# Latent attention software-pipelined over job borders: values two key blocks behind the scores, denominators and reciprocals further behind

## The chip, the cores and the metric

The kernel runs on all 8 cores of one Trainium2 chip. Each core takes one latent sequence of 2048 tokens and four prompts of 256 tokens; no core talks to another. The metric is the device time of the slowest core, in microseconds (us).

A program on all eight cores has a slower state, in which one die (cores 0 to 3, or 4 to 7) or both show a lower granted clock and the time is longer. Each run is marked fast or slow, and only fast runs are compared here.

Engines: PE (TensorE matmul), PEld (its weight loads), DVE (VectorE), ACT (ScalarE), POOL (GpSimd), SP (SyncE). The kernel's helper that issues activations is line 101, so exponentials are the `L101` lines that write the tile `wr`.

## The reference, cut to what matters

Two layers: a gated convolution mixer, then grouped-query attention, each followed by a gated feed-forward part. Only the attention of the latent tokens is touched by most of the change: 8 query heads, 2 key heads, 2560 keys (512 cached, 2048 own).

```python
def one_block(qblk):
    s = jnp.einsum('bqkgd,bskd->bkgqs', qblk, kf) * scale
    p = jax.nn.softmax(s, axis=-1)
    return jnp.einsum('bkgqs,bskd->bqkgd', p, vf)
```

## The kernel before

The program is first recorded as operations with the tiles they read and write. A list scheduler then orders each engine's operations by priority and by a simple model of durations, adds the semaphore waits and emits them. Program order fixes the dependencies. Among ready operations on an engine the lower priority number goes first, and for PE that number grows with program order.

Latent queries are handled in two units of 1024 tokens, S0 (the first unit) and S1 (the second). Each unit has 8 jobs of 2 heads and 512 queries, and each job goes through 20 blocks of 128 keys. Per block: two score matmuls into one of two pairs of banks of PSUM, the memory that matmuls write (banks 0-1 and 2-3), one exponential of 1024 columns on ACT into one of 8 buffers, two value matmuls that accumulate into banks 4-5, and on every second block a pair sum on DVE. The pair sums feed the denominators, matmuls with 32 columns of ones into bank 6.

```python
for hd, q0 in jobs:
    ...
    for c in range(nk):                       # nk = 20 key blocks
        b = 2 * (cnt["set"] % 2)              # two pairs of score banks
        ...
        at(P.prio - 5.0, lambda: P.pe(fs, 2 * MM, ..., pk(b, b + 1)), False)      # scores
        P.act(1024, "ps", pk(b, b + 1), pkk, pt, bank(b, 1024), AF.Exp, scale=att_scale)
        P.pe(fv, 2 * MM, pkk + vbk(c), obk)                                       # values
        if c % 2 == 0: first = (pt, pkk)
        else:
            P.dve(... s = s + pt ...); nb.append((s, sk, c))                      # pair sum
        if c in (5, 11, 19):
            at(P.prio + 1.5, lambda: P.pe(fd, ...), False)                        # denominators
        if c == 3 and pend: pend.pop()()                    # normalise the job before
        yield
    P.dve(... tensor_copy(out=osb, in_=bank(ob, 1024)) ...)     # output copy
    P.dve(... reciprocal(out=rc_t, in_=bank(6, 256)) ...)
    ...                                       # split into two bf16 parts, queue norm_o
```

Other work is woven in. The first unit's attention also carries the key, value and query projections of the second unit. The second unit carries the output projection of the first, then its residual and feed-forward norm.

## Time and profile before

| quantity, kernel before | value | view |
|---|---|---|
| median time | 2576.6 us (2575.7 to 2577.9, 4 runs) | times |
| first unit (first score of S0 to first of S1) | 233.2 us | source view of the score line, median of 8 cores |
| second unit (first to last score of S1) | 228.2 us | same |
| an undisturbed job | 23.7 us | timeline |
| clock | 0.988 to 0.992 | cores view |

From the page: the span, the busy time of each engine, and three rows of the table of 40 equal slices, in which a digit is the busy share in tenths.

```profile
span 2577.6 us, 37681 instructions; the slowest of 8 cores (2564.8 to 2577.6 us)
PE 2387.8 (93%) x12981; PEld 1092.1 (42%) x12981; DVE 1600.2 (62%) x1762; ACT 1342.1 (52%) x1831; POOL 1195.5 (46%) x1114
...
PE   1799999999999999999998998988899999999998
...
DVE  0555686666376818753867787496398628746752
ACT  1233443645257535445777887787644435534433
```

A slice is 64.4 us, so the attention lies in slices 22 to 29, and all but one of the eights in PE's row are there. It does not fill PE, and of the other two engines shown only DVE reaches nine there, in one slice. The windows view says the same in us: four stretches are the program up to the first score, the two units, and the rest; columns are start:end, length, then busy time of PE, PEld, DVE, ACT and POOL with instruction counts, granted clock, DMA share and GB/s.

```profile
0.00:1359.70 1359.70, 1241.94 (x6699) 572.34 (x6700) 800.92 (x885) 641.49 (x956) 704.53 (x673) 0.98 0.55 105
1359.70:1592.90 233.20, 210.72 (x1211) 88.52 (x1210) 183.67 (x226) 183.82 (x217) 75.85 (x62) 0.99 0.25 61
1592.90:1823.50 230.60, 203.33 (x1147) 78.10 (x1146) 153.10 (x211) 181.88 (x205) 45.80 (x39) 1.00 0.06 9
1823.50:2577.60 754.10, 731.77 (x3929) 353.19 (x3927) 462.56 (x442) 334.91 (x455) 369.37 (x340) 0.99 0.51 97
```

ACT is busy 184 of 233 us, then 182 of 231, mostly with exponentials. PE's busy time overstates its work: a single matmul of 512 columns is recorded with 0.38 us and a pair with 0.59, so about 0.16 us of every burst is the tail of its last matmul. Who waits for whom is in the chain of waits followed back from the last instruction, here for the two units, as shares by line:

```profile
by line: PE ps L995 21.6%; PE ps L1003 19.4%; ACT wr L101 17.1%; issue 10.2%; PE ps L856 7.2%; PE ps L598 6.4%; DVE wr L1011 4.0%; PE ps L1017 2.9%; PE ps L916 1.5%; DVE rc L1027 1.5%; DMA wr<-wv 1.1%; PE ps L1041 1.0%; DVE ra L1026 0.7%; D
```

L995 are scores, L1003 values, L1017 denominators. The chain alternates between PE and exponentials, and 10% of it is "issue", time in which the engine waited for nothing that the profile shows. The timeline shows where. These are ACT's lines from an undisturbed stretch near the end of the second unit: start, duration, operation, and in brackets how long ACT had been idle and what ended that.

```profile
1765.59 2.95 ACT L101 ACTIVATE wr<-ps 128x1024 bf16<-128x1024 f32 x3 [0.26 <-PE ps L995]
1769.25 2.95 ACT L101 ACTIVATE wr<-ps 128x1024 bf16<-128x1024 f32 x3 [0.71 <-PE ps L1017]
1772.46 2.95 ACT L101 ACTIVATE wr<-ps 128x1024 bf16<-128x1024 f32 x3 [0.26 <-PE ps L995]
1776.58 1.94 ACT L101 ACTIVATE wr<-ps 128x1024 bf16<-128x1024 f32 x2 [1.17 <-PE ps L995]
1779.35 1.02 ACT L101 ACTIVATE wr<-ps 128x1024 bf16<-128x1024 f32 x1 [0.83 <-PE ps L995]
1780.90 3.85 ACT L101 ACTIVATE wr<-ps 128x1024 bf16<-128x1024 f32 x4 [0.52 <-DVE wr L1011]
```

ACT stops after every three exponentials even in the middle of a job: from 1765.59 to 1772.46 it does 6 in 6.87 us, 1.145 us each. One exponential takes 1.02 us and two in a row take 1.94, so back to back they start 0.92 us apart. (A row of several can hold short waits: in the row of four, 3.85 us, the starts are (3.85 - 1.02) / 3 = 0.943 apart.) At the job border (1776 to 1781) it stops three times more.

PE's lines before the stop at 1772.46 show the queue that the change is aimed at. Four values go first, the next scores start behind them at 1771.71, and ACT, done at 1772.20, waits for these until 1772.46:

```profile
1770.42 0.59 PE L995 MATMUL ps<-ev,ra 128*128 128x512 bf16 x2 [0.31 <-ACT wr L101]
1770.85 1.02 PE L1003 MATMUL ps<-wr,ra 128*128 128x512 bf16 x4
1771.71 1.22 PE L995 MATMUL ps<-ev,ra 128*128 128x512 bf16 x4
```

### The profile page before, as it was taken

The numbers are of one execution on the slowest core, as the hardware profiler recorded it, in microseconds if no ns is written. First come the engines' busy times: TensorE is split into PE (matmuls) and PEld (weight loads), VectorE is DVE, ScalarE is ACT, GpSimd is POOL, SyncE is SP. The second block draws the span as 40 slices with busy tenths as digits, with TensorE's granted clock in tenths as the row PEclk, the third lists the DMA queues.
The fourth block names the chain that finished last, engine by engine and source line by source line (L and its number), as shares of the span: only waits on it lengthen the run. The fifth ranks groups of instructions, "written<-read, shape, count | busy, mean of one in ns | idle before, by whom it ended". The sixth has DMA issues, their size and how long they took to land.

```text
span 2577.6 us, 37681 instructions; the slowest of 8 cores (2564.8 to 2577.6 us)
## 1 busy us (share of the span) xinstructions
PE 2387.8 (93%) x12981; PEld 1092.1 (42%) x12981; DVE 1600.2 (62%) x1762; ACT 1342.1 (52%) x1831; POOL 1195.5 (46%) x1114
## 2 busy tenths in 40 slices
PE   1799999999999999999998998988899999999998
PEld 0344444444444444444444433333344444444446
DVE  0555686666376818753867787496398628746752
ACT  1233443645257535445777887787644435534433
POOL 2137462945266547455362433320344546546434
PEclk9999999999999999999999999999999999999999
DMA  9456746365476545544333400100345356538621
GB/s 181 94 103 141 161 85 108 66 105 93 73 157 139 114 82 99 107 79 90 66 59 88 120 13 9 29 1 1 66 77 88 67 113 129 123 68 170 115 51 66
DMA packets 75226, 231.92 MB, mean 90 GB/s; under 512 B 9248, under 2 KB 14880, under 8 KB 75040
## 3 DMA queue, kind: packets, MB, share of 16 engines
q0 software_dynamic: 48512, 170.55, 39.2%
q1 hardware_dynamic: 26528, 58.98, 7.1%
q8 instruction: 107, 1.75, 0.3%
q14 instruction: 79, 0.65, 0.1%
HBM read 370.65 MB, written 29.36 MB: 155 GB/s over the span
## 4 chain that ended last, share of the span: by engine, by line
PE 77%; issue 6%; DVE 5%; ACT 5%; DMA 5%; POOL 1%; another core or an unknown queue 1%; SPq 0%; ACTq 0%; DVEq 0%; POOLq 0%
PE ps L665 39%; PE ps L598 24%; PE ps L995 4%; PE ps L1003 3%; ACT wr L101 3%; PE ps L856 3%; DMA h<-x_in 2%; DMA wr<-win 2%; PE ps L916 1%; PE ps L496 1%; DVE wr L1011 1%; PE ps L672 1%; DVE ev L690 1%; DMA h<-h_mem 1%
## 5 line engine op out<-in xcount | busy, mean ns | idle before, releaser
L665 PE MATMUL ps<-u,wr 128*128 128x512 bf16 x5376 | 1196.4, 382 | 33.3 <-DMA wr<-win 15.0
L665 PEld LDWEIGHTS ps<-u,wr 128*128 128x128 bf16 x5376 | 519.2, 98 | 654.6 <-issue 57.0
L690 DVE SCALAR_TENSOR_TENSOR ev<-ps,par,ev 128x1023 f32<-128x1023 f32 (+1 forms) x336 | 429.0, 1281 | 161.9 <-ACT ev L101 129.1
L598 PE MATMUL ps<-ra,wr 128*128 128x512 bf16 (+1 forms) x2338 | 514.4, 381 | 16.1 <-DVE ra L727 6.2
L101 ACT ACTIVATE wr<-ps 128x1024 bf16<-128x1024 f32 (+1 forms) x352 | 332.1, 989 | 72.7 <-PE ps L995 46.0
L598 PEld LDWEIGHTS ps<-ra,wr 128*128 128x128 bf16 x2338 | 230.1, 99 | 294.5 <-issue 31.1
L101 ACT ACTIVATE ev<-ps,par 128x1024 f32<-128x1024 f32 x168 | 186.8, 1112 | 222.2 <-PE ps L665 220.7
L690 DVE SCALAR_TENSOR_TENSOR ra<-ps,par,ra 128x1023 f32<-128x1023 f32 (+1 forms) x192 | 242.9, 1277 | 38.5 <-ACT ra L101 24.5
L770 POOL TENSOR_TENSOR ra<-ev 128x1023 bf16<-128x1023 f32 (+1 forms) x84 | 198.3, 2361 | 141.2 <-ACT ev L101 67.8
L490 POOL TENSOR_TENSOR rs<-rs,sqb 128x512 f32<-128x512 f32 (+1 forms) x125 | 177.1, 1425 | 134.9 <-ACT sqb L101 133.7
L1011 DVE TENSOR_TENSOR wr<-wr 128x1024 bf16<-128x1024 bf16 x160 | 136.5, 857 | 127.7 <-PE ps L1003 126.4
L101 ACT ACTIVATE ra<-ps,par 128x1024 f32<-128x1024 f32 x96 | 106.6, 1112 | 124.3 <-PE ps L665 93.8
L1003 PE MATMUL ps<-wr,ra 128*128 128x512 bf16 x640 | 169.9, 380 | 1.5 <-ACT wr L101 1.5
L578 DVE SCALAR_TENSOR_TENSOR yb<-yb,coef,ps 128x512 f32<-128x512 f32 (+1 forms) x72 | 49.2, 683 | 190.3 <-ACT ps L101 187.4
L535 DVE SCALAR_TENSOR_TENSOR tm<-h,coef,rs 128x512 f32<-128x512 f32 x176 | 150.1, 886 | 21.1 <-ACT rs L101 21.1
L101 ACT ACTIVATE yb<-ps 128x512 f32<-128x512 f32 (+1 forms) x120 | 68.3, 569 | 179.7 <-PE ps L598 178.9
L101 ACT ACTIVATE sqa<-h 128x512 bf16<-128x512 f32 x152 | 92.3, 626 | 115.2 <-DMA h<-x_in 61.4
L578 DVE SCALAR_TENSOR_TENSOR ev<-ev,coef,ps 128x512 f32<-128x512 f32 x72 | 53.3, 741 | 156.9 <-ACT ps L101 155.0
L101 ACT ACTIVATE sqb<-ps 128x512 bf16<-128x512 f32 (+1 forms) x219 | 127.7, 585 | 40.5 <-PE ps L856 17.4
L101 ACT ACTIVATE ev<-ps 128x512 f32<-128x512 f32 x80 | 47.5, 597 | 172.3 <-PE ps L598 172.3
L770 POOL TENSOR_TENSOR ra<-ra 128x1023 bf16<-128x1023 f32 (+1 forms) x48 | 114.1, 2377 | 39.9 <-ACT ra L101 24.7
L490 POOL TENSOR_TENSOR rs<-rs,sqa 128x512 f32<-128x512 f32 x80 | 96.3, 1204 | 69.1 <-ACT sqa L101 51.7
(179 smaller groups left out, 2661.9 us busy)
## 6 DMA issues: line engine op xcount, KB each, us to landing
wr<-wup POOLq DMA_DIRECT2D x132, 512.0 KB, 6.4
wr<-wdn POOLq DMA_DIRECT2D x41, 704.0 KB, 6.5
wr<-modw POOLq DMA_DIRECT2D x40, 512.0 KB, 6.3
wr<-win POOLq DMA_DIRECT2D x24, 768.0 KB, 9.2
h_mem<-h SPq DMA_DIRECT2D x24, 512.0 KB, 6.2
h<-h_mem SPq DMA_DIRECT2D x24, 512.0 KB, 7.2
h_out<-h SPq DMA_DIRECT2D x40, 256.0 KB, 7.2
h<-x_in SPq DMA_DIRECT2D x16, 512.0 KB, 9.9
```

Of the source, the lines that this page charges most:

```text
L101: return self._add("act", lambda e: e.activation(out=out, in_=in_, func=func, **kw), reads, writes, busy, busy + 0.12, table=self.TABLES.g ...
L490: fn = lambda e, o=o, a=a, s=s: e.tensor_tensor(out=o, in0=a, in1=s, op=ALU.add)
L535: P.dve(lambda e, kc=kc, t=t, rs=rs, src=hap(U, kc, ct * 512, ct * 512 + 512): e.scalar_tensor_tensor(out=t, in0=src, scalar=cf[:, ai, kc, ...
L578: fy = lambda e, y=y, m=m: e.scalar_tensor_tensor(out=y, in0=y, scalar=cf[:, gi, m, U.v:U.v + 1], in1=rs, op0=ALU.mult, op1=ALU.mult)
L598: ins = e.matmul(bank(b, n), w3[:, k, :], rhs(k), start=(k == 0), stop=(k == nk - 1))
L665: ins = e.matmul(bank(b + ct), lhs_fn(kc), ub.ap[:, kc, ct * 512:ct * 512 + 512], start=(kc == 0), stop=(kc == KC - 1))
L690: P.dve(lambda e, ro=ro, zi=zi, w=w: e.scalar_tensor_tensor(out=ro, in0=zi, scalar=w, in1=ro, op0=ALU.mult, op1=ALU.add), 1024, rd + wr, w ...
L770: P.pool(lambda e, rg=rg, ru=ru, c=c: e.tensor_tensor(out=a3(c, c0, c1), in0=rg[:, c0:c1], in1=ru[:, c0:c1], op=ALU.mult), 1024, rgk + ruk ...
L856: ins = e.matmul(bank(b), w3[:, kc, :], ub.ap[:, kc, ct * 512:ct * 512 + 512], start=(kc == 0), stop=(kc == KC - 1))
L995: ins = e.matmul(bank(b + a), kt[:, j, c * 128:c * 128 + 128], qbuf.ap[:, hd + a, q0:q0 + 512], start=True, stop=True)
L1003: ins = e.matmul(bank(ob + a), vb[:, c, j * 128:(j + 1) * 128], pt[:, a * 512:(a + 1) * 512], start=(c == 0), stop=(c == nk - 1))
L1011: P.dve(lambda e, s=s, pt=pt: e.tensor_tensor(out=s, in0=s, in1=pt, op=ALU.add), 512, sk + pkk, sk, sh=True)
```

## The change

The intent: a block's values are issued two blocks after its scores, when the exponential they need has long been done, and the pipeline does not stop at job borders. Denominators come 5 blocks, reciprocals 6 and normalisation 10 blocks later. A shared dependency key, `("qk",)`, written by scores and read by values and denominators, fixes the order of these on PE: scores(i), values(i-2), scores(i+1), and so on. Three further edits: the output copy and the border's value matmuls are split by bank, one norm sums its squares on PE instead of DVE, and the scheduler's model of the delay from any other engine to PE (DMA apart) falls from 0.4 to 0.2 us.

```diff
-                lag = 0.0 if (s.eng == e == "pe") else (0.4 if s.eng == "pe" and not o.nbytes else 0.06)
+                lag = 0.0 if (s.eng == e == "pe") else (0.2 if s.eng == "pe" and not o.nbytes else 0.06)
 ... (one more cut: a norm helper takes its engine by name; same effect as before)
+            def scores(I):
 ...
+                P.pe(fs, 2 * MM, ktk(...) + J.qk, pk(b, b + 1) + [("qk",)])
+                P.act(1024, "ps", pk(b, b + 1), I.pk, I.pt, bank(b, 1024), AF.Exp, scale=att_scale)
+            def values(I):
+                for h in ((0,), (1,)) if c in (0, nk - 1) else ((0, 1),):
+                    ...
+                    P.pe(fv, len(h) * MM, I.pk + vbk(c) + [("qk",)], pk(*[ob + a for a in h]))
 ... (pair sum as before, but written over the odd block)
+            def denominators(J):
+                nb, J.sums = J.sums[:2], J.sums[2:]
+                ...
+                P.pe(fd, 0.22 + 0.11 * len(nb), [...] + [("ones",), ("qk",)], pk(6))
+            def copy_out(J):
+                for a in range(2):
+                    P.dve(... tensor_copy(out=J.osb[:, a * 512:a * 512 + 512], in_=bank(ob + a)) ...)
 ... (recip, norm_o: the operations of before)
+            n = len(items)                       # all blocks of all 8 jobs
+            for i in range(n + 11):
+                if i < n:
+                    scores(items[i])
+                if 0 <= i - 2 < n:
+                    I = items[i - 2]
+                    values(I)
+                    if I.c == nk - 1:
+                        copy_out(I.J)
+                for lag, cs, fn in ((5, (3, 7, 11, 15, 19), denominators), (6, (19,), recip), (10, (19,), norm_o)):
+                    if 0 <= i - lag < n and items[i - lag].c in cs:
+                        fn(items[i - lag].J)
+                yield
 ...
-        steps(g, 22)
+        steps(g, 28)
         run(wo_out(S0, UU, ...))
-        steps(g, 42)
-        at(P.prio + 30.0, lambda: norm(S0, 1, 2, 3, UU, bk=7, sq="pool", on_dve=True), False)
+        steps(g, 36)
+        at(P.prio + 30.0, lambda: norm(S0, 1, 2, 3, UU, bk=7, sq="pool", groups=range(KC)), False)
```

More of the change, by code (lines that the diff above doesn't have):

```diff
@@ L497, in sumsq, with norm @@
                      sk + [("ones",)], pk(b))
-        def norm(U, l, ai, bpart, ub, bk=5, pool_act=False, **kw):
+        def norm(U, l, ai, bpart, ub, bk=5, on=None, **kw):
             for ct in range(2):
                 norm_stats(U, ct, bk, **kw)
-                norm_apply(U, ct, l, ai, bpart, ub, pool_act)
+                norm_apply(U, ct, l, ai, bpart, ub, on)
         def norm_stats(U, ct, bk=5, sq="act", groups=(0, 7), on_dve=False):
@@ L514, in norm_stats, with norm_apply @@
             rstd_ops(bk, 512, rs, [("rs", ct)])
-        def norm_apply(U, ct, l, ai, bpart, ub, pool_act=False):
+        def norm_apply(U, ct, l, ai, bpart, ub, on=None):
             mv, cf = mvs[l], cfs[l]
@@ L526, in norm_apply @@
                     o, ok = ub.ap[:, kc, ct * 512:ct * 512 + 512], ub.keys(kc, ct * 512, ct * 512 + 512)
-                if pool_act:
+                if on:
                     P.pool(lambda e, t=t, rs=rs, src=hap(U, kc, ct * 512, ct * 512 + 512): e.tensor_tensor(
                         out=t, in0=src, in1=rs, op=ALU.mult), 512, hk(U, kc, ct) + [("rs", ct)], tk)
-                    P.act(512, "sb", tk + [("mod", l, bpart, U.v), ("coef", l, ai, U.v)], ok, o, t, AF.Identity,
-                          bias=mv[:, bpart * 8 + kc, U.v:U.v + 1], scale=cf[:, ai, kc, U.v:U.v + 1])
+                    shift, scale = mv[:, bpart * 8 + kc, U.v:U.v + 1], cf[:, ai, kc, U.v:U.v + 1]
+                    if on == "act":
+                        P.act(512, "sb", tk + [("mod", l, bpart, U.v), ("coef", l, ai, U.v)], ok, o, t, AF.Identity, bias=shift, scale=scale)
+                    else:
+                        P.pool(lambda e, t=t, o=o, shift=shift, scale=scale: e.tensor_scalar(
+                            out=o, in0=t, scalar1=scale, scalar2=shift, op0=ALU.mult, op1=ALU.add), 220,
+                            tk + [("mod", l, bpart, U.v), ("coef", l, ai, U.v)], ok)
                     if ub is None:
@@ L971, in attend @@
         def attend(U, qbuf, osbs):
-            jobs = [(hd, qt * 512) for qt in range(2) for hd in range(0, 8, 2)]
             ob, nk, npt = 4, 20, 8
             pt0 = WR - 2 * npt
-            pend = []
-            obk = pk(ob, ob + 1)
-            for hd, q0 in jobs:
-                j = hd // 4
-                qk = [q for a in range(2) for q in qbuf.keys(hd + a, q0, q0 + 512)]
-                nb = []
+            class Item:
+                pass
+            class Job:
+                pass
@@ new lines, in attend @@
+            jobs = []
+            for qt in range(2):
+                for hd in range(0, 8, 2):
+                    J = Job()
+                    J.hd, J.j, J.q0, J.sums = hd, hd // 4, qt * 512, []
+                    J.qk = [q for a in range(2) for q in qbuf.keys(hd + a, J.q0, J.q0 + 512)]
+                    jobs.append(J)
+            items = []
+            for J in jobs:
+                for c in range(nk):
+                    I = Item()
+                    I.J, I.c = J, c
+                    items.append(I)
@@ new lines, in scores, with fs @@
+            def scores(I):
+                J, c = I.J, I.c
+                cnt["set"] += 1
+                b = 2 * (cnt["set"] % 2)
+                cnt["pt"] = (cnt["pt"] + 1) % npt
+                pb = pt0 + 2 * cnt["pt"]
+                I.pt, I.pk = wr_t[:, pb * 512:pb * 512 + 1024], [("w", pb), ("w", pb + 1)]
+                def fs(e):
+                    for a in range(2):
+                        ins = e.matmul(bank(b + a), kt[:, J.j, c * 128:c * 128 + 128], qbuf.ap[:, J.hd + a, J.q0:J.q0 + 512], start=True, stop=True)
+                    return ins
+                P.pe(fs, 2 * MM, ktk(J.j, c * 128, c * 128 + 128) + J.qk, pk(b, b + 1) + [("qk",)])
+                P.act(1024, "ps", pk(b, b + 1), I.pk, I.pt, bank(b, 1024), AF.Exp, scale=att_scale)
@@ new lines, in values, with fv @@
+            def values(I):
+                J, c = I.J, I.c
+                for h in ((0,), (1,)) if c in (0, nk - 1) else ((0, 1),):
+                    def fv(e, h=h):
+                        for a in h:
+                            ins = e.matmul(bank(ob + a), vb[:, c, J.j * 128:(J.j + 1) * 128], I.pt[:, a * 512:(a + 1) * 512],
+                                           start=(c == 0), stop=(c == nk - 1))
+                        return ins
+                    P.pe(fv, len(h) * MM, I.pk + vbk(c) + [("qk",)], pk(*[ob + a for a in h]))
+                if c % 2 == 0:
+                    J.first = (I.pt, I.pk)
+                else:
+                    s, sk = J.first
+                    P.dve(lambda e: e.tensor_tensor(out=I.pt, in0=s, in1=I.pt, op=ALU.add), 512, sk + I.pk, I.pk, sh=True)
+                    J.sums.append((I.pt, I.pk, c))
@@ new lines, in denominators, with fd @@
+            def denominators(J):
+                nb, J.sums = J.sums[:2], J.sums[2:]
+                def fd(e):
+                    for s, _, c in nb:
+                        for g in range(4):
+                            ins = e.matmul(ps[32 * g:32 * g + 32, 6 * 512:6 * 512 + 256], ones_h[:, 0:32],
+                                           s[:, g * 256:(g + 1) * 256], start=(c == 1), stop=(c == nk - 1))
+                    return ins
+                P.pe(fd, 0.22 + 0.11 * len(nb), [q for x in nb for q in x[1]] + [("ones",), ("qk",)], pk(6))
@@ L983, in attend @@
+            def copy_out(J):
                 cnt["o"] = (cnt["o"] + 1) % len(osbs)
                 obt, obn, o0 = osbs[cnt["o"]]
-                osb, osk = obt[:, o0 // 4:o0 // 4 + 1024], A(obn, o0, o0 + 4096)
-                for c in range(nk):
-                    cnt["set"] += 1
-                    b = 2 * (cnt["set"] % 2)
-                    cnt["pt"] = (cnt["pt"] + 1) % npt
-                    pb = pt0 + 2 * cnt["pt"]
-                    pt, pkk = wr_t[:, pb * 512:pb * 512 + 1024], [("w", pb), ("w", pb + 1)]
-                    def fs(e, b=b, c=c, hd=hd, j=j, q0=q0):
-                        for a in range(2):
-                            ins = e.matmul(bank(b + a), kt[:, j, c * 128:c * 128 + 128], qbuf.ap[:, hd + a, q0:q0 + 512], start=True, stop=True)
-                        return ins
-                    at(P.prio - 5.0, lambda: P.pe(fs, 2 * MM, ktk(j, c * 128, c * 128 + 128) + qk, pk(b, b + 1)), False)
-                    P.prio += 2 * MM
-                    P.act(1024, "ps", pk(b, b + 1), pkk, pt, bank(b, 1024), AF.Exp, scale=att_scale)
-                    def fv(e, pt=pt, c=c, j=j):
-                        for a in range(2):
-                            ins = e.matmul(bank(ob + a), vb[:, c, j * 128:(j + 1) * 128], pt[:, a * 512:(a + 1) * 512],
-                                           start=(c == 0), stop=(c == nk - 1))
-                        return ins
-                    P.pe(fv, 2 * MM, pkk + vbk(c), obk)
-                    if c % 2 == 0:
-                        first = (pt, pkk)
-                    else:
-                        s, sk = first
-                        P.dve(lambda e, s=s, pt=pt: e.tensor_tensor(out=s, in0=s, in1=pt, op=ALU.add), 512, sk + pkk, sk, sh=True)
-                        nb.append((s, sk, c))
-                    if c in (5, 11, 19):
-                        def fd(e, nb=tuple(nb)):
-                            for s, _, c in nb:
-                                for g in range(4):
-                                    ins = e.matmul(ps[32 * g:32 * g + 32, 6 * 512:6 * 512 + 256], ones_h[:, 0:32],
-                                                   s[:, g * 256:(g + 1) * 256], start=(c == 1), stop=(c == nk - 1))
-                            return ins
-                        at(P.prio + 1.5, lambda: P.pe(fd, 0.22 + 0.11 * len(nb), [q for x in nb for q in x[1]] + [("ones",)], pk(6)), False)
-                        P.prio += 0.22 + 0.11 * len(nb)
-                        nb = []
-                    if c == 3 and pend:
-                        pend.pop()()
-                    yield
@@ L1026, in attend, with recip @@
-                P.dve(lambda e, osb=osb: e.tensor_copy(out=osb, in_=bank(ob, 1024)), 1024, obk, osk)
-                P.dve(lambda e: e.reciprocal(out=rc_t, in_=bank(6, 256)), 256 * 6.4, pk(6), [("rc",)])
+                J.osb, J.osk = obt[:, o0 // 4:o0 // 4 + 1024], A(obn, o0, o0 + 4096)
+                for a in range(2):
+                    P.dve(lambda e, a=a: e.tensor_copy(out=J.osb[:, a * 512:a * 512 + 512], in_=bank(ob + a)), 512, pk(ob + a), J.osk[2 * a:2 * a + 2])
+            def recip(J):
@@ L1028, in attend @@
                 cnt["rc"] = 1 - cnt["rc"]
                 hi, hl = hl_t[:, 0:256], hl_t[:, (cnt["rc"] + 1) * 256:(cnt["rc"] + 2) * 256]
-                hik, hlk = [("hi",)], [("hl", cnt["rc"])]
-                P.dve(lambda e, hi=hi: e.tensor_copy(out=hi, in_=rc_t), 128, [("rc",)], hik, sh=True)
-                P.dve(lambda e, hl=hl, hi=hi: e.scalar_tensor_tensor(
-                    out=hl, in0=hi, scalar=par[:, P_SPLIT:P_SPLIT + 1], in1=rc_t, op0=ALU.mult, op1=ALU.add), 256,
-                    hik + [("rc",), ("par",)], hlk, sh=True)
@@ L1036, in norm_o @@
-                def norm_o(hl=hl, hlk=hlk, osb=osb, osk=osk, hd=hd, q0=q0):
-                    for a in range(2):
-                        def fb(e, a=a):
-                            for g in range(2):
-                                gg = 2 * a + g
-                                ins = e.matmul(bank(7, 256, g * 256), sel_t[:, gg * 128:(gg + 1) * 128], hl, start=True, stop=True)
-                            return ins
-                        P.pe(fb, 2 * 0.11, hlk + [("sel",)], pk(7))
-                        P.dve(lambda e, a=a: e.tensor_tensor(
-                            out=qbuf.ap[:, hd + a, q0:q0 + 512], in0=osb[:, a * 512:a * 512 + 512], in1=bank(7), op=ALU.mult),
-                            512, osk + pk(7), qbuf.keys(hd + a, q0, q0 + 512))
@@ L1047, in attend @@
-                pend.append(norm_o)
-            pend.pop()()
-            yield
+                hik, J.hlk = [("hi",)], [("hl", cnt["rc"])]
+                J.hl = hl
+                P.dve(lambda e: e.reciprocal(out=rc_t, in_=bank(6, 256)), 256 * 6.4, pk(6), [("rc",)])
+                P.dve(lambda e: e.tensor_copy(out=hi, in_=rc_t), 128, [("rc",)], hik, sh=True)
+                P.dve(lambda e: e.scalar_tensor_tensor(
+                    out=hl, in0=hi, scalar=par[:, P_SPLIT:P_SPLIT + 1], in1=rc_t, op0=ALU.mult, op1=ALU.add), 256,
+                    hik + [("rc",), ("par",)], J.hlk, sh=True)
@@ new lines, in norm_o, with fb @@
+            def norm_o(J):
+                for a in range(2):
+                    def fb(e, a=a):
+                        for g in range(2):
+                            gg = 2 * a + g
+                            ins = e.matmul(bank(7, 256, g * 256), sel_t[:, gg * 128:(gg + 1) * 128], J.hl, start=True, stop=True)
+                        return ins
+                    P.pe(fb, 2 * 0.11, J.hlk + [("sel",)], pk(7))
+                    P.dve(lambda e, a=a: e.tensor_tensor(
+                        out=qbuf.ap[:, J.hd + a, J.q0:J.q0 + 512], in0=J.osb[:, a * 512:a * 512 + 512], in1=bank(7), op=ALU.mult),
+                        512, J.osk + pk(7), qbuf.keys(J.hd + a, J.q0, J.q0 + 512))
@@ L1128, in build_program @@
               (mod_gen(1, [1, 0]), 4, 1.6), lead=4.0)
-        at(P.prio + 60.0, lambda: norm(S1, 1, 0, 0, None, bk=7, groups=range(KC), pool_act=True), False)
+        at(P.prio + 60.0, lambda: norm(S1, 1, 0, 0, None, bk=7, groups=range(KC), on="act"), False)
         stage(ffn_in(PU, 0, UU, False), ffn_out(PU, 0), [lambda: norm(S0, 0, 2, 3, UU)],
```

## The prediction

> **What bounds the kernel now.** The page gives PE 93% busy over 2577.6 us; most of that is feed-forward and projection stages, hardly touched by the change. Latent attention runs from about 1360 to 1824 us (source view of the score and value matmuls); there no engine is full: the windows view gives, per 40 us, PE 33 to 38, ACT 29 to 34, DVE 17 to 39.
>
> In the timeline of its undisturbed end one job (2 heads, 512 queries, 20 key blocks) takes 23.7 us, from the output copy at 1776.28 to that at 1800.02. Estimated from the same view, PE needs 80 matmuls of 0.2165 us, 40 denominator matmuls (1.4) and 4 broadcasts (0.4): 19.2 us. ACT needs 20 exponentials, 0.963 apart back to back (3.85 for four): 19.3 us. The Trainium skill, "ScalarE: Activation LUTs", What ACT_TABLE_LOAD costs, gives 186 ns + 0.833 ns per element less 93 ns overlap, 0.946 us for 1024 columns: it agrees. PE and ACT are balanced; the other 4.4 us are handshakes: scores wait for ACT to empty their bank, ACT waits for scores, and at each job border values wait for the 1.22 us output copy (ACT idle 1.2, 0.8 and 0.5 us there).
>
> **What the change does.** The PE order becomes scores(i), values(i-2), fixed by a common dependency; both need only the exponential of block i-2, so scores no longer queue behind values of the newest one. From the trace, exponential end to score start is 0.2 us, two matmuls 0.59, hand-back 0.1: 0.89, under the 0.963 of the other bank's exponential, so ACT can run nearly without gaps. The border copy is cut into two 0.68 us halves (estimated bubble left: 0.7 us). Denominators come five times, not three; reciprocal (1.75 us on DVE) and normalisation move off the border. Twelve DVE adds of one norm become matmuls. New: a rigid PE order, where a late pair sum on DVE stops scores too, and a drain of 2 to 3 us between the two latent units. The scheduler's smaller hand-off lag reorders the rest: within 5 us.
>
> **What it is worth.** Pure job: about 20.9 us (19.3 ACT, 0.7 border, 0.65 denominators, 0.2 broadcasts), saving nearly 3; from 1650 to 1824 us some 140 blocks run: 24 to 28 us. The first unit (1360 to 1600) also carries projections: PE about 200 of 240 us, DVE 190, so these limit it: 15 to 18 us. The output projection woven in at 1612 to 1650 is PE bound: little. The Trainium skill, "SBUF — State Buffer", SBUF: two separate sides, describes DVE and GpSimd blocking each other on a shared port; here pair sums stretch from 0.69 to 4.1 us, so not all DVE slack is usable. Drain and reordering cost 0 to 5. Total about 45 us, on the critical path, where PE and ACT alternate.
>
> Predicted 2532 us, 8 in 10 between 2504 and 2563. Faster by over 2%: 0.40; within 2%: 0.57; slower: 0.03.
>
> **What would show it.** Attention shortens from 464 to about 420 us; the pure job to about 21; ACT idle before exponentials falls by over half; DVE's output copies are 32 of 0.68 us; feed-forward stages keep their lengths within 1 to 2 us each.
>
> **What would make it wrong.** Late DVE sums or copies stalling the rigid PE chain in the first unit (PE waiting over 10 us on DVE); projection blocks of 1.73 us starving ACT as before; the lag change moving feed-forward stages by 10 us or more, either way.

## The result, and the profile after

The median is 2537.1 us (fast runs 2533.4 to 2537.2; a fourth, slow run took 2564.0) against 2576.6 before. The ratio is 0.9842, with a 95% interval of 0.9822 to 0.9861. A ratio here is the mean time of one kernel's fast runs over that of the other's of the same rounds, so it is not quite the ratio of the medians. The change saves 40 us, 1.6%, which counts as within 2%.

The page after, its first two rows:

```profile
span 2536.1 us, 37659 instructions; the slowest of 8 cores (2526.7 to 2536.1 us)
PE 2376.2 (94%) x12993; PEld 1090.1 (43%) x12993; DVE 1575.6 (62%) x1766; ACT 1344.0 (53%) x1833; POOL 1199.9 (47%) x1114
```

Busy times have hardly moved. What moved is the length of two stages; the windows view after, in the same four stretches:

```profile
0.00:1358.80 1358.80, 1236.90 (x6702) 570.56 (x6703) 796.62 (x885) 644.16 (x960) 707.64 (x673) 0.99 0.56 105
1358.80:1579.10 220.30, 209.83 (x1234) 87.70 (x1235) 185.96 (x238) 182.78 (x215) 79.01 (x64) 1.00 0.25 64
1579.10:1783.00 203.90, 197.62 (x1142) 79.18 (x1139) 136.92 (x201) 178.03 (x200) 43.26 (x40) 1.00 0.07 10
1783.00:2536.10 753.10, 731.87 (x3923) 352.65 (x3920) 456.06 (x443) 339.07 (x459) 370.03 (x338) 0.99 0.51 97
```

The first unit is 12.9 us shorter, the second 26.7; the parts ahead and behind differ by 1 us each. All the gain is in the attention. The chain of waits through it:

```profile
by line: PE ps L1012 33.6%; PE ps L1022 30.9%; PE ps L862 7.5%; PE ps L1039 6.1%; PE ps L604 5.3%; ACT wr L101 3.3%; issue 2.5%; PE ps L922 1.7%; PE ps L1067 1.5%; DMA wr<-wv 1.3%; DMA wr<-wo 1.0%; DVE wr L1030 1.0%; DVE ra L1049 0.8%; PE p
```

L1012 are now the scores, L1022 the values, L1039 the denominators. Exponentials fell from 17% of the chain to 3%, and "issue" from 10% to 2.5%: the chain now runs along PE. ACT's timeline of one undisturbed job after:

```profile
1740.35 1.94 ACT L101 ACTIVATE wr<-ps 128x1024 bf16<-128x1024 f32 x2 [0.22 <-PE ps L1012]
1742.91 1.94 ACT L101 ACTIVATE wr<-ps 128x1024 bf16<-128x1024 f32 x2 [0.62 <-PE ps L1012]
1745.08 3.85 ACT L101 ACTIVATE wr<-ps 128x1024 bf16<-128x1024 f32 x4 [0.22 <-PE ps L1012]
1749.15 3.88 ACT L101 ACTIVATE wr<-ps 128x1024 bf16<-128x1024 f32 x4 [0.22 <-PE ps L1012]
1753.27 3.89 ACT L101 ACTIVATE wr<-ps 128x1024 bf16<-128x1024 f32 x4 [0.23 <-PE ps L1012]
1757.38 3.85 ACT L101 ACTIVATE wr<-ps 128x1024 bf16<-128x1024 f32 x4 [0.22 <-PE ps L1012]
1761.45 1.94 ACT L101 ACTIVATE wr<-ps 128x1024 bf16<-128x1024 f32 x2 [0.22 <-PE ps L1012]
1764.02 1.94 ACT L101 ACTIVATE wr<-ps 128x1024 bf16<-128x1024 f32 x2 [0.62 <-PE ps L1012]
```

Now ACT runs four exponentials without a gap, then waits 0.22 us, once for each group of denominators; at the border it waits 0.62 us once. A job takes 21.1 us (1742.91 to 1764.02), 2.6 less. PE's side of the first gap and of the border:

```profile
1738.79 0.59 PE L1022 MATMUL ps<-wr,ra 128*128 128x512 bf16 x2
1739.31 0.40 PE L1039 MATMUL ps<-wr,ones_h 128*32 128x256 bf16 x8
1739.64 0.61 PE L1012 MATMUL ps<-ev,ra 128*128 128x512 bf16 x2
...
1741.41 0.38 PE L1022 MATMUL ps<-wr,ra 128*128 128x512 bf16 x1 [0.30 <-DVE ra L1049]
1742.01 0.38 PE L1022 MATMUL ps<-wr,ra 128*128 128x512 bf16 x1 [0.22 <-DVE ra L1049]
```

From the start of values to the start of the next scores is 0.85 us instead of 0.43, so the eight denominator matmuls cost PE 0.42 us. ACT's gap of 0.22 us comes once with each such group. At the border the two value matmuls wait 0.30 and 0.22 us for the halves of the output copy.

One more gap is new. Between the units ACT is idle for 2.75 us (2.75 to 3.4 on the eight cores). The fixed order lets no score of the second unit start before the last denominators of the first, and these wait for their pair sum on DVE:

```profile
1578.75 0.40 PE L1039 MATMUL ps<-wr,ones_h 128*32 128x256 bf16 x8 [2.28 <-DVE wr L1030]
1579.79 2.88 ACT L101 ACTIVATE wr<-ps 128x1024 bf16<-128x1024 f32 x3 [2.75 <-PE ps L1012]
```

### The profile page after: what moved, and what is told of

The parts are those of the page before. It is cut to its first block, busy times and chain, and to the rows that moved or that the text cites. A ratio compares the mean times of both kernels' runs of the same rounds, so it can differ in the third digit from the quotient of the medians.

```text
span 2536.1 us, 37659 instructions; the slowest of 8 cores (2526.7 to 2536.1 us)
## 1 busy us (share of the span) xinstructions
PE 2376.2 (94%) x12993; PEld 1090.1 (43%) x12993; DVE 1575.6 (62%) x1766; ACT 1344.0 (53%) x1833; POOL 1199.9 (47%) x1114
## 4 chain that ended last, share of the span: by engine, by line
PE 78%; DMA 5%; DVE 5%; issue 5%; ACT 4%; POOL 2%; SPq 1%; DVEq 0%; ACTq 0%; POOLq 0%
PE ps L671 37%; PE ps L604 24%; PE ps L1012 6%; PE ps L1022 5%; DMA h<-x_in 2%; PE ps L862 2%; DMA wr<-win 1%; DVE ra L696 1%; PE ps L1039 1%; SPq L115 1%; PE ps L496 1%; ACT yb L101 1%; PE ps L922 1%; ACT wr L101 1%; PE ps L678 1%
## 5 line engine op out<-in xcount | busy, mean ns | idle before, releaser
L101 ACT ACTIVATE wr<-ps 128x1024 bf16<-128x1024 f32 (+1 forms) x352 | 329.1, 987 | 44.4 <-PE ps L1012 43.8
L1022 PE MATMUL ps<-wr,ra 128*128 128x512 bf16 x640 | 192.2, 379 | 4.9 <-DVE ra L1049 2.6
L115 POOL DMA_DIRECT2D wr<-wup x132 | 76.6, 581 | 108.5 <-PE ps L496 37.8
```

The costliest lines, as they stand in the source:

```text
L101: return self._add("act", lambda e: e.activation(out=out, in_=in_, func=func, **kw), reads, writes, busy, busy + 0.12, table=self.TABLES.g ...
L115: return self._add(q, lambda e: e.dma_start(out=out, in_=in_, **kw), reads, writes, 0.55 if q == "pool" else 0.65, 0.0, nbytes=nbytes, rat ...
L1022: ins = e.matmul(bank(ob + a), vb[:, c, J.j * 128:(J.j + 1) * 128], I.pt[:, a * 512:(a + 1) * 512], start=(c == 0), stop=(c == nk - 1))
```

## The experiments

Twelve kernels ran; all are on record as correct (but see e_order_only). Each was compared with the kernel before on its own chip, where that took 2579 to 2590 us in its fast runs, somewhat more than on the first chip. Stage lengths of different chips are compared with each other; those of the kernel before are from the first chip. The stage lengths are medians over the 8 cores of the profiled run, by the source view of the score line: first unit, then second unit.

| kernel | fast runs, us | ratio to before (95% interval) | first unit | second unit | undisturbed job |
|---|---|---|---|---|---|
| before | 2575.7 to 2577.9 | 1 | 233.2 | 228.2 | 23.7 |
| changed | 2533.4 to 2537.2 | 0.9842 (0.9822 to 0.9861) | 220.2 | 200.9 | 21.1 |
| e_order_only | 2559.1, 2579.5 (2 of 5) | none | 230.6 | 208.2 | 21.5 |
| e_lag_only | 2568.3 to 2578.0 | 0.9966 (0.9945 to 0.9986) | 233.0 | 223.2 | |
| e_values1 | 2580.3 to 2582.0 | 0.9995 (0.9977 to 1.0013) | 240.4 | 221.7 | 23.75 |
| e_drain | 2544.6, 2547.9 (2 of 4) | 0.9860 (0.9838 to 0.9881) | 220.8 | 204.1 | 21.6 |
| e_nolag | 2616.3, 2618.7 (2 of 5) | 1.0131 (1.0102 to 1.0159) | 262.2 | 239.7 | 25.9 |
| e_onecopy | 2542.4 to 2547.8 | 0.9850 (0.9820 to 0.9881) | 223.7 | 202.0 | 21.5 |
| e_oldnorm | 2543.1 to 2548.7 | 0.9854 (0.9831 to 0.9878) | 220.3 | 208.5 | |
| e_noorder | 2533.6 to 2540.0 | 0.9820 (0.9796 to 0.9844) | 219.3 | 199.1 | 20.55 |
| e_lag04 | 2547.1 (1 of 3) | none | 222.2 | 199.8 | |
| e_order_lags | 2556.3, 2559.0 (2 of 3) | 0.9895 (0.9853 to 0.9938) | 224.2 | 209.7 | |
| e_noorder_quads | 2553.6 to 2561.3 | 0.9896 (0.9867 to 0.9925) | 222.3 | 217.8 | 21.4 |
| e_noorder_units | 2535.4 to 2555.8 | 0.9838 (0.9803 to 0.9874) | 218.2 | 199.6 | |

Two theories stood against each other first. A: the gain is the hand-off inside a job, since scores no longer queue behind values of the newest exponential. B: the gain is what left the job border, as the change's name suggests. A third, C, was the scheduler's smaller hand-off lag.

### e_order_only: only the order of scores and values

```diff
 (from the changed kernel)
-  lag 0.2; copy in two halves; norm with groups=range(KC)
+  lag 0.4; one copy of 1024 columns, values undivided; norm with on_dve=True
-  nb, J.sums = J.sums[:2], J.sums[2:]
+  nb, J.sums = J.sums, []
-  P.pe(fd, ..., [...] + [("ones",), ("qk",)], pk(6))
+  at(P.prio + 1.5, lambda: P.pe(fd, ..., [...] + [("ones",)], pk(6)), False)
-  for lag, cs, fn in ((5, (3, 7, 11, 15, 19), denominators), (6, (19,), recip), (10, (19,), norm_o)):
+  for lag, cs, fn in ((2, (5, 11, 19), denominators), (2, (19,), recip), (6, (19,), norm_o)):
-  steps(g, 28) ... steps(g, 36)
+  steps(g, 24) ... steps(g, 40)
```

The two step counts move so that the output projection, whose sums share PSUM bank 6 with the denominators, still falls between two jobs' denominators.

> Only the order of scores and values of the changed kernel, everything else put back (one output copy, three denominator groups without lag and outside the rigid order, reciprocal at the border, old norm on DVE, old hand-off lag). Theory A (the gain is the hand-off inside a job, scores no longer behind values of the newest exponential): at least 70% of the 40 us, so 2543 to 2552 us, and an undisturbed job near 22 us (23.7 before, 21.1 after). Theory B (the gain is what left the job border): under half of it, 2560 us or more. Theory C (the smaller hand-off lag of the scheduler): nothing, 2577.

It gave neither number. Of its two runs marked fast, the profiled one took 2559.1 us, 24 less than the kernel before on that chip (median of fast runs 2582.9). The other took 2579.5, with one die at a clock of 0.973 to 0.986. So the stage lengths carry the weight. The two units shorten by 22.6 us of the 40.3 that the change saves there: 2.6 in the first, 20.0 in the second. In the undisturbed job the order alone gives 2.2 of the 2.6 us, as A says. In the first unit it gives almost nothing. What it left there is seen in the waits of ACT and PE during that unit (engine, line, what it waited for: us in total, times, longest):

```profile
ACT wr L101 <- PE ps L1012: 20.0, 22, 1.8
ACT wr L101 <- PE ps L1039: 14.5, 17, 2.0
...
PE ps L1022 <- DVE yb L1049: 6.9, 7, 1.4
```

The same lines of the changed kernel, whose first unit has no wait of ACT behind denominators (L1039) at all:

```profile
ACT wr L101 <- PE ps L1012: 27.5, 37, 2.2
...
PE ps L1022 <- DVE yb L1049: 2.1, 6, 0.8
```

So with the order alone two things hold up the first unit: the denominators in groups of 12 and 16, and the undivided copy. ACT's waits behind denominators fit the 8 buffers: an exponential may not overwrite a pair sum that denominators still have to read.

The run has a flaw. The last denominators of a job are recorded after the exponential of block 1 of the next job, and that exponential takes the buffer with the sum of blocks 12 and 13. So in 14 of the 16 jobs they read the exponential instead of the sum, and the softmax denominators are not those of the reference. In the right order this exponential would have had to wait for them, so the run may flatter the order alone. e_order_lags (below) has the same order without the flaw, an undisturbed job of 21.5 us too, and 209.7 us for the second unit.

### e_lag_only: only the scheduler's hand-off lag

```diff
 (from the kernel before)
-  lag = ... (0.4 if s.eng == "pe" and not o.nbytes else 0.06)
+  lag = ... (0.2 if s.eng == "pe" and not o.nbytes else 0.06)
```

> The kernel before with the scheduler's hand-off lag of 0.2 alone. Theories A and B: within 5 us of 2577. Theory C: 2560 or less.

The ratio of 0.9966 is about 9 us (95% interval 4 to 14), where A and B expected at most 5; the units account for 5.2 of them. C as the main cause falls. In the changed kernel the same number is worth less (e_lag04, below).

### e_values1: values one block behind the scores

```diff
-                if 0 <= i - 2 < n:
-                    I = items[i - 2]
+                if 0 <= i - 1 < n:
+                    I = items[i - 1]
```

> The changed kernel with values one block behind the scores, not two. Theory A: scores(i+1) queue behind values(i-1), which wait for the exponential of block i-1, so hand-off 0.2 + values 0.43 + scores 0.59 + 0.1 = 1.32 us against the other exponential's 0.963: ACT idle about 0.3 to 0.36 us per block, an undisturbed job of 26 to 28 us, the whole kernel 2590 to 2630 us, slower than before. Theory B: it keeps most of the gain, 2537 to 2550, since all border work still lags.

The whole gain is gone: 0.9995, an undisturbed job of 23.75 us, as before. B, for which this kernel should have kept most of the gain, falls here. A's direction holds, but its size was about twice too big. ACT's timeline shows why:

```profile
1770.91 2.01 ACT L101 ACTIVATE wr<-ps 128x1024 bf16<-128x1024 f32 x2 [0.28 <-PE ps L1012]
1773.20 2.06 ACT L101 ACTIVATE wr<-ps 128x1024 bf16<-128x1024 f32 x2 [0.28 <-PE ps L1012]
```

The gap comes once in two blocks, not once in each. The loop runs through one pair of score banks, and each pair serves every second block. The pieces, from the trace: exponential 1.02 us, until the values that wait for it start 0.15, values 0.43, scores 0.59, back to ACT 0.10. That is 2.29 us, and from 1770.91 to 1773.20 it is 2.29. A block then takes 2.29 / 2 = 1.145 us, the same as in the kernel before. Without the values the loop is 1.86 us, about what two exponentials back to back need (1.84). The expectation had set the loop against one exponential instead of two.

### e_drain: the same pipeline, emptied at every job border

```diff
                     items.append(I)
+                items.extend([None, None])        # two steps without scores after each job
 (the loop skips None; the woven steps become 30 and 40)
```

> The changed kernel drained at every job border: no score of the next job before the last values of this one; denominators, reciprocals and normalisation still lag. Theory A: each of 16 borders costs about 0.7 to 1.3 us more (exponential, hand-off, values, scores in series, while the output copy is then partly hidden), so 10 to 18 us: 2547 to 2555. Theory B: most of the gain goes, 2560 or more.

The units take 424.9 us together, 3.8 more than changed, less than A's 10 to 18. At the border ACT waits 1.26 us instead of 0.62, but the copy is then hidden and one denominators' gap is missing in exchange:

```profile
1749.76 2.88 ACT L101 ACTIVATE wr<-ps 128x1024 bf16<-128x1024 f32 x3 [1.26 <-PE ps L1013]
1752.92 5.82 ACT L101 ACTIVATE wr<-ps 128x1024 bf16<-128x1024 f32 x6 [0.28 <-PE ps L1013]
```

Letting scores and values run over the border is worth only about a tenth of the gain. This is the second result against B, though the work that lags over the border still lagged here.

### Second round: where the rest of the gain is

From here A became A2: the order gives the undisturbed job its gain, and the lags give what the first unit gained, because DVE is busy and late there. B2: the rest came from copies, norm or the scheduler's lag.

### e_nolag: border work without its lags

```diff
-  ((5, (3, 7, 11, 15, 19), denominators), (6, (19,), recip), (10, (19,), norm_o)):
+  ((2, (3, 7, 11, 15, 19), denominators), (2, (19,), recip), (6, (19,), norm_o)):
 (woven steps 24 and 40, for the reason given above)
```

> The changed kernel without the lags of the border work: denominators right behind the pair sum they read, reciprocal right behind the last of them, normalisation four blocks sooner; order of scores and values, split copies, norm and hand-off lag as changed. Theory A2 (the order gives the undisturbed job, the lags give what the mixed first unit gained, because there VectorE is busy and late): first unit (first score of one unit to the first of the next) back to 228 to 233 us (220.2 changed, 230.6 with the order alone), second unit 205 to 210 (200.9 changed), 2550 to 2558 us in all. Rival B2 (the rest came from split copies, norm or hand-off lag): first unit 220 to 223, in all within 5 us of the changed kernel.

Far worse than either expected: 1.3% slower than before, and both units are longer than in the kernel before. PE's timeline:

```profile
1799.06 0.40 PE L1039 MATMUL ps<-wr,ones_h 128*32 128x256 bf16 x8 [0.95 <-DVE wr L1030]
1799.39 0.60 PE L1012 MATMUL ps<-ev,ra 128*128 128x512 bf16 x2
```

In a fixed order each group of denominators waits about 0.95 us for the pair sum that DVE has just begun, and the scores behind it wait too: PE waits 75.2 us for pair sums in all (72 times), 2.7 in the changed kernel. The lag is what makes the fixed order affordable. By itself this does not say what the lags gave over the kernel before, which had no fixed order; e_order_lags does.

### e_onecopy, e_oldnorm, e_lag04: one edit undone each

```diff
 e_onecopy: -  for h in ((0,), (1,)) if c in (0, nk - 1) else ((0, 1),):   and two copies of 512
            +  for h in ((0, 1),):                                         and one copy of 1024
 e_oldnorm: -  norm(S0, 1, 2, 3, UU, bk=7, sq="pool", groups=range(KC))
            +  norm(S0, 1, 2, 3, UU, bk=7, sq="pool", on_dve=True)
 e_lag04:   -  0.2 if s.eng == "pe" ...
            +  0.4 if s.eng == "pe" ...
```

> The changed kernel with one 1024-column output copy per job and undivided value matmuls at the border. Theory A2: a border bubble of 0.9 to 1.2 us on ACT instead of 0.62, so 4 to 9 us over 16 borders, 2541 to 2547. Rival B2: 10 us or more, most of it in the first unit.

> The changed kernel with the feed-forward norm of the first unit as it was (pair adds on VectorE in place of matmuls). Theory A2: 2 to 5 us in the second unit only, the first unit unchanged. Rival B2: over 7 us.

> The changed kernel with the old hand-off lag of 0.4 in the scheduler, all else as changed. If the lag is a matter of tuning only: first and second unit within 3 us of the changed kernel (220.2 and 200.9). If it carries what the other single removals have not explained of the first unit (order alone 230.6, one copy 223.7): first unit 224 or more.

One copy costs 4.6 us in the units (3.5 + 1.1), within what A2 expected. ACT's border gap in the undisturbed job is 1.00 us instead of 0.62:

```profile
1750.14 1.94 ACT L101 ACTIVATE wr<-ps 128x1024 bf16<-128x1024 f32 x2 [0.22 <-PE ps L1012]
1753.07 1.94 ACT L101 ACTIVATE wr<-ps 128x1024 bf16<-128x1024 f32 x2 [1.00 <-PE ps L1012]
```

The old norm costs 7.6 us, all in the second unit: more than A2's 2 to 5, and within what B2 said (over 7). Those 12 adds take DVE time in the very stretch where it also does the residual and the pair sums, and PE waits 5.4 us for pair sums in that unit, in one case 5.1 us:

```profile
PE ps L1039 <- DVE wr L1030: 5.4, 2, 5.1
PE ps L1022 <- DVE ra L1049: 4.6, 14, 0.8
```

The old scheduler lag costs 0.9 us in the units (2.0 more in the first, 1.1 less in the second): tuning, as expected.

### e_order_lags: the account between the order alone and the whole change

```diff
 (from the changed kernel: the edits of e_onecopy, e_oldnorm and e_lag04 together)
```

> The order of scores and values and all lags of the border work as changed, but one output copy, the old norm and the old hand-off lag. Closes the account between the order alone (230.6 and 208.2 us for the units) and the changed kernel (220.2 and 200.9). If the parts add up: first unit 224 to 227 (one copy +3.5, hand-off lag +2), second 207 to 210 (norm +7.6, one copy +1.1), so the lags are worth about 5 us of the first unit and nothing of the second. If they do not add up, first unit 220 to 223 or 228 and more.

The parts add up, 224.2 and 209.7. Stepwise, in us of first and second unit:

| step | first unit | second unit | both |
|---|---|---|---|
| order of scores and values (before to e_order_only) | -2.6 | -20.0 | -22.6 |
| lags and five groups, in the fixed order (to e_order_lags) | -6.4 | +1.5 | -4.9 |
| split copies, norm on PE, scheduler lag (to changed) | -4.0 | -8.8 | -12.8 |
| sum | -13.0 | -27.3 | -40.3 |

The single removals of the last step are 4.6, 7.6 and 0.9 us, 13.1 together against 12.8.

So A2 is only partly right. Of the 17.7 us beyond the order, the lags gave 4.9 and the three edits of B2 gave 12.8; in the first unit it is 6.4 against 4.0. The split between the first two steps is the less certain part, since it rests on the flawed e_order_only.

### e_noorder: without the common dependency

```diff
-  ... pk(b, b + 1) + [("qk",)]      ... vbk(c) + [("qk",)]      ... [("ones",), ("qk",)]
+  ... pk(b, b + 1)                  ... vbk(c)                  ... [("ones",)]
```

> The changed kernel without the common dependency that fixes the PE order; program order and lags stay, and the scheduler orders as it likes (it then puts scores and values in fours, two blocks at a time). Theory A2: it loses the alternation and most of the undisturbed job's gain: second unit 212 to 222 us, in all 2550 to 2565. Rival D (lagging the program is enough, the scheduler finds a good order by itself): within 5 us of the changed kernel.

A2's expectation falls and rival D holds. The scheduler mostly finds the alternation by itself from the program order. Of 257 unbroken runs of scores on the profiled core (other work left out), 215 are one block's two matmuls; the other 42, of four to ten, are spread over both units, and in the last 40 us they lie at job borders only. It may also move a score ahead of a value that waits for the copy, and so the border gap goes, as ACT's timeline shows:

```profile
1743.22 5.82 ACT L101 ACTIVATE wr<-ps 128x1024 bf16<-128x1024 f32 x6 [0.28 <-PE ps L1012]
1749.31 1.94 ACT L101 ACTIVATE wr<-ps 128x1024 bf16<-128x1024 f32 x2 [0.27 <-PE ps L1012]
```

Six exponentials run over the border (near 1745) without a gap. The job takes 20.55 us, and the units 418.4, 2.7 less than changed. In the time this cannot be told from the changed kernel (0.9820 and 0.9842, intervals that overlap, on two chips). So the key thing is the recorded program order with its lags; the fixed order itself is not needed, and by the stage lengths costs a little.

### e_noorder_quads and e_noorder_units: two attempts at more

```diff
 e_noorder_quads: on every fourth block DVE adds two pair sums; a denominator group reads that one sum
 e_noorder_units: attend() takes both units, one list of 320 blocks, so nothing drains between them
```

> The changed kernel without the common dependency (219.3 and 199.1 us for the units), with sums of four exponentials on VectorE, so that each denominator group has 4 matmuls, not 8. If the 0.22 us of ACT idle after each group is their cost on the critical path: second unit 4 to 8 us shorter. The added VectorE work (5 adds of 0.69 us a job, where VectorE is about 85% busy in the first unit) may cost the first unit 0 to 8 us. In all 2530 to 2545.

> The changed kernel without the common dependency and with one pipeline through both latent units, so that nothing drains between them. The drain showed as 2.75 us of ACT idle between the units, so 2 to 4 us less over both units together (418.4 without the common dependency, 421.1 changed); in all 2525 to 2538, hardly to be told in the time.

Sums of four lost 21.7 us against e_noorder, 18.7 of them in the second unit, where 4 to 8 us were to be gained. DVE, at 136 of 201 us in the changed kernel's second unit, is at 181 of 218 here, and 62 of 67 in its last stretch (columns as in the windows view above):

```profile
1740.00:1807.00 67.00, 63.98 (x326) 25.20 (x332) 61.56 (x102) 60.28 (x63) 0.00 (x0) 0.98 0.00 1
```

The gaps of ACT did not shrink either; 0.24 us is still seen after a group. Whether they would with DVE free is open, because the scheduler's order changed as well.

One pipeline over both units gave 417.8 us for the units, 0.6 less than e_noorder, not 2 to 4. (Its profiled run is the slowest of its four, with a clock of 0.976 on two cores, but the stage lengths of the cores agree within 1 us.) The expectation had the wrong base: e_noorder has no drain left to remove. Without the key, the first score of the second unit starts at 1583.39, ahead of the last denominators of the first at 1586.69, and within 8 us of that border ACT is idle for over 0.3 us at a time on none of its cores. So what the drain costs in time was not measured by itself; the 2.7 us that e_noorder gained hold it and the border gaps together. No version beats the changed kernel by more than the noise of the time.

## Why the prediction was right, point by point

- **The time.** 2532 us was predicted, 2504 to 2563 in 8 of 10 cases; 2537.1 was measured. The chance given to "within 2%", where the result lies, was 0.57.
- **What bounds the kernel.** Right in kind: hand-offs, not a full engine. e_values1 shows it most plainly: one block less of distance, everything else kept, and the gain is gone. The balance of 19.2 us (PE) and 19.3 us (ACT) a job was a little off. The 0.963 us is a row of four, 3.85 us from first start to last end, divided by four; at 0.92 from start to start, ACT needs about 18.5 us. PE needs 17.3 for scores and values, 0.4 for broadcasts (the matmuls of the normalisation) and, at the measured 0.42 a group, 2.1 for denominators: 19.9 us in the changed kernel. So PE is now the fuller engine, as the chain says.
- **The undisturbed job.** 20.9 predicted, 21.1 measured. Of the terms, the border was sized well (0.7; 0.62 measured). The denominators were not: 0.65 predicted, 5 gaps of 0.22, so 1.1 us, measured. The sum still comes close, in part because 19.3 is 0.8 us more than exponentials need back to back, which makes room for short waits. Groups of 4, 8 and 12 matmuls cost PE 0.32, 0.42 and 0.54 us between values and what follows, so about 0.2 us is paid per group, whatever its size. The 0.2 for broadcasts was too much: 3.88 instead of 3.85 for the four exponentials around one.
- **The second unit.** 24 to 28 us predicted, 27.3 measured, but partly by luck. Seven jobs at "nearly 3" us come to some 20, which is what the order gave (20.0); the prediction does not say where the rest of its 24 to 28 was to come from. In the runs it came mostly from the norm on PE, 7.6 us by its removal, which the prediction names ("Twelve DVE adds of one norm become matmuls") and gives no worth.
- **The first unit.** 15 to 18 predicted, 13.0 measured. The reason given, projections that fill PE and a busy DVE, fits, but no run isolates it: the order gives 2.6 us there, the lags 6.4 and the other edits 4.0. The danger that projection blocks starve ACT "as before" was real: ACT waits for scores 27.5 us in this unit after the change and 27.1 before.
- **Reordering.** "Within 5 us" holds in the changed kernel (0.9 us by e_lag04). In the kernel before the same number alone is worth about 9 us in time (interval 4 to 14) and 5.2 in the units. The parts outside the attention moved by 1 us each, as predicted.
- **The signs named in advance.** The attention went from 464 to 424 us (420 predicted); the output copies are 32 of 0.68 us; PE waits for DVE 4.8 us in the first unit, under the 10 named as a danger. One sign failed: ACT's idle time before exponentials, on the page's group of 352, fell from 72.7 to 44.4 us, 39% and not "over half". In the undisturbed job it did fall by more than half (4.3 to 1.7 us a job, adding up the gaps in ACT's record).
- **The rigid order** was listed as a risk. e_nolag shows the risk was real, and that the lags remove it; e_noorder shows that it was not needed.
- **The drain between the units** was predicted at 2 to 3 us and seen as 2.75 us of idle ACT. Its cost in time stays open: e_noorder removed it only together with the border gaps, 2.7 us in all.

## What to carry to other kernels

Where two engines hand work back and forth through two buffers, count the whole loop of one buffer in us (here exponential 1.02, on to the scores 0.15, scores 0.59, back 0.10: 1.86 for two blocks, against 1.84 for two exponentials back to back) and let nothing else sit inside it: values issued one block behind the scores instead of two put 0.43 us into the loop and cost 2.6 us a job here. Record side work far enough behind that its inputs are surely ready before an in-order engine meets it: denominators right behind their sums made the same pipeline, in a fixed order, slower than no pipeline at all. And when a change bundles edits, price each alone: a one-line norm edit was a fifth of this gain, and the running over job borders that names the change about a tenth.

## What the Trainium skill lacked or had wrong

- "TensorEngine Tiling (Array Packing)", Key Properties: it says that switching the tiling mode drains TensorE; that section has no figure for it. Here groups of 4, 8 and 12 matmuls of 128x32 weights and 256 columns between full-size matmuls cost 0.32, 0.42 and 0.54 us: about 0.1 us per four, what one full-size matmul of 256 columns takes here (0.11), as tiles that work in parallel should, and about 0.2 us more per group. That fits the drain, but no run isolates it.
- "Perfetto Trace Analysis", Per-instruction lifecycle: it says that semaphore propagation lies outside the reported windows; that section has no figure for it. Here 0.15 us pass from the recorded end of an exponential to the start of the scores that waited for it, and 0.10 us from the recorded end of scores to the start of the exponential (matmul ends are modelled in this profile, so the second figure is less sure).
- "ScalarE: Activation LUTs", What ACT_TABLE_LOAD costs: estimated from its figures, an exponential of 1024 columns takes 1.04 us alone and 0.946 us back to back; measured were 1.02 and 0.92 us (1.94 for two), 2 to 3% less.
- "SBUF — State Buffer", SBUF: two separate sides: it describes the lock between VectorE and GpSimd but not what it costs a kernel. Here the pair sums took 0.62 to 2.95 us in the changed kernel's first unit, where GpSimd is busy 79 of 220 us, and 0.63 to 0.69 us in the last 43 us of its attention, where GpSimd is busy 1.4 us. This fits the page; no experiment separated the lock from other causes.
